# Weight pieces of 1024 columns with two split ahead, in place of pieces of 512 columns with five split ahead

## The chip, the cores and the metric

The kernel runs on one core of one Trainium2 chip. The metric is the device time of one execution in microseconds (us); less is better. TensorE is PE in the profile, VectorE DVE, ScalarE ACT, GpSimd POOL, and SP issues the DMAs.

## The reference

Three residual blocks are applied one after the other to `x` of 256 tokens by 2048 features, all in fp32. What matters here is that each is a long row of products of 256 tokens with big weight matrices, with smaller work between them:

```python
# block 1: gated convolution, gated linear attention (GLA), attention over 256 memory rows
proj = rmsnorm(x) @ w_in                        # 2048 x 19472, cut into 11 parts
y = g0 * (conv @ w_conv_out) + g1 * (gla @ w_gla_out) + g2 * (mem @ w_mem_out)
x = rmsnorm(x + y @ w_out, final_g)
# block 2: sparse attention with a learned top-k, spatial gating, a feed-forward part of 8192
x = x + (...) @ w_out_2
x = rms_norm(x + gelu(rms_norm(x) @ w_ff1) @ w_ff2, final_g_2)
# block 3: latent attention (MLA) and a bidirectional RWKV-7 scan, gated and merged
out = x + rms_norm((...) @ w_out_3, g_post)
```

## The kernel before

**The stream.** All weights of the three blocks lie in DRAM as one stream, in the order in which they are used (`stream_plan`). `cut` cuts each product into pieces: a piece is `n` chunks of 128 rows by `w` columns (512 as a rule), with `n = min(nk, ITEM // w)`; `ITEM` is the number of columns that a piece takes in each partition. Pieces are packed into units of up to `UNIT = 1024` columns (512 KB); one DMA brings one unit into one of `RAW = 4` buffers `raw`.

**The split.** PE multiplies in a fast fp32 form that keeps fewer bits, so each fp32 operand is split into a high and a low part and three products are made: high by high, low by high, high by low. For each piece ACT copies `raw` to `wh` (the high part), and then DVE computes `wl = raw - wh`. The activations were split earlier, into `xh` and `xl` (`yr`, `qa`, `kv` and others in some products). A chunk of 128 x 512 weights then takes 6 matmuls of 512 columns on PE (3 products for 2 halves of the tokens), or 12 of 256 columns in products whose output is wanted transposed (`DIRECT`).

**What runs ahead.** `run_stream` goes through the pieces. At the start of piece `i` it writes the splits up to piece `i + LEAD` into the programs of ACT and DVE, then the evacuation of the product that just ended (`finish`), then the matmuls of piece `i`. `wh` and `wl` come from a pool of `LEAD + 1` buffers each, so the split of piece `i + LEAD` goes into the buffer that piece `i - 1` has just left:

```python
        self.w_p = pool("w", LEAD + 1)
...
            while ns < len(items) and ns <= i + min(LEAD, 1 + i):
...
                wh = self.w_p.tile([128, ITEM], F32R, name="wh", tag="wh")
                wl = self.w_p.tile([128, ITEM], F32R, name="wl", tag="wl")
                nc.scalar.activation(out=wh[:, :size], in_=src, func=AF.Copy)
                nc.vector.tensor_tensor(
                    out=wl[:, :size], in0=src, in1=wh[:, :size].bitcast(F32), op=ALU.subtract
                )
...
            self.finish(over)
```

**The side work.** Everything else (norms, convolution, attention, scans) consists of generators. Between the matmuls `pump` takes a step of each generator that is due. A clock kept by the program at build time (`Issue`), with a cost for each instruction, says what is due; `BACKLOG` bounds how far ACT and DVE may fall behind PE in it. Each engine runs its program strictly in the order in which it was written, so a split stands behind all side work and evacuations that were written before it.

Names used below: `wo` is the last product of block 1, `wo2` the output product of block 2's first part, `f20` to `f23` the feed-forward's second product, `wo3` the last product; `bm`, `br0` and `br1` are the merging products of block 3. Four column blocks (0 to 3) make one product of 2048 columns. The evacuations of `wo` and of `f23` add the residual, and per half of the tokens DVE adds, ACT squares and sums (`junk`), DVE multiplies by a gain row and ACT squares and sums again.

Of the kernel before, what the change touches and what calls it, by code (L numbers as in the profile page):

```python
# [16 lines left out]
AX = mybir.AxisListType  # L17
D = 2048
EPS = 1e-6
ITEM = 512  # L20
UNIT = 1024
NSLOT = 13
RAW = 4
COMMON = ("ev", "sg", "row", "junk", "rsq", "rsz", "ss")
BEGIN = {"qi": 2, "qa": 3}
EXTRA = {1: 0, 2: 0, 3: 1}
LEAD = 5
BACKLOG = 7.7
TABLES = {AF.Exp: ("exp", "ln"), AF.Ln: ("ln",), AF.Sigmoid: ("sigmoid",), AF.Silu: ("silu",), AF.Sqrt: ("sqrt",),
          AF.Gelu_apprx_tanh: ("gelu",), AF.Tanh: ("exp", "sigmoid", "silu", "gelu")}  # L30
# [87 lines left out]
def cut(plan):  # L118

    items, units, off = [], [], 0  # L120
    for key, j, src, row0, nk, col0, w in plan:
        n = min(nk, ITEM // w)
        for k in range(0, nk, n):
# [174 lines left out]
class Builder:  # L298
    def __init__(self, ctx, tc, dram, blocks):
# [7 lines left out]
        self.raw_p = pool("raw", RAW)  # L307
        self.w_p = pool("w", LEAD + 1)
        self.wk = pool("work")
# [183 lines left out]
    def run_stream(self):  # L493
# [5 lines left out]
        for i, it in enumerate(items):  # L499
            self.cur = f"{it.key}{it.j}"  # L500
            opens = it.key in BEGIN and it.first and it.j == 0
            if opens:
                self.finish(over)
                over = None
                self.begin(BEGIN[it.key])
            while ns < len(items) and ns <= i + min(LEAD, 1 + i):
                jt = items[ns]
                while nd < len(units) and nd <= jt.unit + RAW - 1:
                    off, size = units[nd]
                    t = self.raw_p.tile([128, UNIT], F32, name="raw", tag="raw")  # L510

                    m = size if nd else min(size, ITEM)
                    src = wfl[off:off + 128 * size].rearrange("(p n) -> p n", p=128)
# [7 lines left out]
                src = raw[jt.unit][:, jt.uoff:jt.uoff + size]  # L521
# [3 lines that stand above are left out]
# [2516 lines left out]
```

## Time and profile before

| | |
|---|---|
| median of 3 runs | 3540.02 us (3539.14 to 3540.11) |
| the profiled execution | 3546.78 us, span 3545.0 us |
| PE busy | 3506.3 us, 99% of the span |
| DVE busy | 2442.9 us, 69% |
| ACT busy | 1893.6 us, 53% |
| POOL busy | 158.8 us, 4% |
| mean granted PE clock | 0.994 of full speed |
| HBM | 661.74 MB read, 36.73 MB written, 197 GB/s |

The span reaches from the first instruction to the last; the profiled execution has 1.8 us beside it. Busy is the time in which an engine executed something. Consecutive matmuls overlap in the records, so their spacing, not their duration, is what one costs.

### The profile page before, as it was taken

What the parts mean: (1) busy time and instruction counts of PE and PEld (TensorE: products, weight loads), DVE (VectorE), ACT (ScalarE), POOL (GpSimd) and SP (SyncE); (2) the same over time, 40 slices, a digit from 0 to 9 for tenths busy, and PEclk for the clock granted to TensorE, in tenths of its full rate; (3) what the DMA queues carried; (4) which work ended last, traced back from release to release, by engine and by line L of the source; (5) the groups of instructions that cost most, each with busy time, mean ns of one, the idle gap of its engine ahead of it and who ended that gap; (6) DMA issues with size and microseconds to landing.
All of it is one profiled execution on the core that took longest, in us unless ns stands there. A gap on an engine that the chain in (4) does not pass through costs nothing.

```text
span 3545.0 us, 55751 instructions
## 1 busy us (share of the span) xinstructions
PE 3506.3 (99%) x20370; PEld 3036.2 (86%) x20370; DVE 2442.9 (69%) x4447; ACT 1893.6 (53%) x3398; POOL 158.8 (4%) x153
## 2 busy tenths in 40 slices
PE   8999999999999999999999999999999999999998
PEld 7889988888988899988878989898988997787777
DVE  7598898887576666555766555555567578678785
ACT  6555556556454555655445545454555664464444
POOL 1000010001000000100110000000000010000010
PEclk9999999999999999999999999999999999999999
DMA  6555656676677765566665555555575456655665
GB/s 230 169 188 161 188 158 208 193 232 194 181 231 221 239 207 189 178 214 224 215 225 184 185 191 185 194 184 192 187 222 175 147 183 191 217 188 189 230 215 183
DMA packets 235995, 698.98 MB, mean 197 GB/s; under 512 B 44932, under 2 KB 55348, under 8 KB 234056
## 3 DMA queue, kind: packets, MB, share of 16 engines
q1 hardware_dynamic: 235720, 695.43, 60.9%
q8 instruction: 159, 2.61, 0.3%
q14 instruction: 116, 0.95, 0.1%
HBM read 661.74 MB, written 36.73 MB: 197 GB/s over the span
## 4 chain that ended last, share of the span: by engine, by line
PE 91%; DVE 5%; DMA 2%; issue 1%; ACT 1%; SPq 0%; POOL 0%; DVEq 0%; ACTq 0%
PE acc L285 84%; PE bank L285 7%; DVE wl L285 2%; DVE tmp L285 1%; DMA raw<-in_wstream_dram 1%; DVE m L285 0%; ACT wh L285 0%; DMA x<-f 0%; DMA tl<-td 0%; DVE tl L285 0%; DVE rb L285 0%; ACT junk L285 0%; DVE o L285 0%; DVE xl L285 0%; DMA row<-in_rows_dram 0%
## 5 line engine op out<-in xcount | busy, mean ns | idle before, releaser
L285 DVE TENSOR_TENSOR wl<-raw,wh 128x512 fp32r<-128x512 f32 x2290 | 1568.8, 702 | 993.9 <-ACT wh L285 977.1
L285 ACT ACTIVATE wh<-raw 128x512 fp32r<-128x512 f32 x2290 | 1424.2, 630 | 1503.7 <-PE acc L285 936.1
L285 PE MATMUL acc<-wh,xh 128*128 128x512 f32 x3328 | 1324.7, 398 | 11.3 <-ACT xh L285 4.5
L285 PE MATMUL acc<-wh,xl 128*128 128x512 f32 x3328 | 1299.7, 391 | 3.9 <-DVE xl L285 3.9
L285 PE MATMUL acc<-wl,xh 128*128 128x512 f32 x3328 | 1298.8, 390 | 1.2 <-DVE wl L285 1.2
L285 PEld LDWEIGHTS acc<-wh,xh 128*128 128x128 f32 x3328 | 627.5, 189 | 145.9 <-issue 11.9
L285 PEld LDWEIGHTS acc<-wh,xl 128*128 128x128 f32 x3328 | 627.0, 188 | 137.3 <-DVE xl L285 4.7
L285 PEld LDWEIGHTS acc<-wl,xh 128*128 128x128 f32 x3328 | 628.3, 189 | 129.9 <-DVE wl L285 7.0
L285 PE MATMUL acc<-xh,wh 128*128 128x256 f32 (+3 forms) x2224 | 637.7, 287 | 0.0
L285 PE MATMUL acc<-xh,wl 128*128 128x256 f32 (+3 forms) x2224 | 629.6, 283 | 0.0
L285 PE MATMUL acc<-xl,wh 128*128 128x256 f32 (+3 forms) x2224 | 629.6, 283 | 0.0
L285 PEld LDWEIGHTS acc<-xh,wh 128*128 128x128 f32 (+3 forms) x2224 | 423.9, 191 | 3.2 <-issue 2.0
L285 PEld LDWEIGHTS acc<-xl,wh 128*128 128x128 f32 (+3 forms) x2224 | 424.1, 191 | 1.3
L285 PEld LDWEIGHTS acc<-xh,wl 128*128 128x128 f32 (+3 forms) x2224 | 423.8, 191 | 0.4
L285 DVE SCALAR_TENSOR_TENSOR cacc<-u,cvec,cacc 128x226 f32<-128x226 f32 (+28 forms) x464 | 188.5, 468 | 0.0
L285 ACT ACT_TABLE_LOAD x46 | 59.0, 1283 | 3.2 <-DVE mmx L285 1.6
L285 PE MATMUL acc<-wh,yr 128*128 128x512 f32 x128 | 43.7, 410 | 2.0 <-DVE yr L285 2.0
L285 ACT ACTIVATE junk<-x 128x512 bf16<-128x512 f32 x40 | 25.3, 632 | 37.1 <-DVE x L285 36.7
L285 PE MATMUL bank<-ar,bk 64*128 64x128 f32 (+1 forms) x384 | 40.4, 329 | 0.1
L285 POOL TENSOR_TENSOR crstd<-crstd,u 128x256 f32<-128x256 f32 x14 | 21.9, 1561 | 356.5 <-DVE u L285 356.0
L285 PEld LDWEIGHTS bank<-ar,bk 64*128 64x128 f32 x384 | 25.6, 186 | 14.2 <-issue 10.0
L285 POOL MEMSET ropes<- 64x256 f32 x2 | 0.6, 306 | 727.3 <-DVE wl L285 727.2
(427 smaller groups left out, 2205.2 us busy)
## 6 DMA issues: line engine op xcount, KB each, us to landing
raw<-in_wstream_dram SPq DMA_DIRECT2D x1133, 512.0 KB, 3.9
gate<-sg SPq DMA_DIRECT2D x40, 256.0 KB, 2.3
row<-in_rows_dram SPq DMA_DIRECT2D x38, 256.0 KB, 4.8
sg<-gate SPq DMA_DIRECT2D x24, 256.0 KB, 2.9
sg<-z SPq DMA_DIRECT2D x24, 256.0 KB, 2.6
z<-sg SPq DMA_DIRECT2D x20, 256.0 KB, 2.5
f<-x SPq DMA_DIRECT2D x16, 256.0 KB, 2.5
gt<-gate SPq DMA_DIRECT2D x16, 256.0 KB, 4.3
```

Source lines behind the costliest of these rows:

```text
L285: r = f(*a, **k)
```

## The change

`ITEM` goes from 512 to 1024 and `LEAD` from 5 to 2. A piece of a 512-column product is now 2 chunks, takes one ACT and one DVE instruction of 1024 columns, and holds 12 matmuls of 512 columns (24 of 256). The `wh` and `wl` buffers are 3 each of 1024 columns in place of 6 each of 512: the same space. Units, `raw` buffers and matmuls stay as they are. One more place reads `ITEM`: the first unit was loaded by two DMAs of 512 columns each and is now loaded by one.

```diff
-ITEM = 512
+ITEM = 1024
 UNIT = 1024
 NSLOT = 13
 RAW = 4
...
-LEAD = 5
+LEAD = 2
 BACKLOG = 7.7
```

DVE, at the evacuation of `wo`'s column block 0 (`acc` is the product in PSUM, `x` the new residual, `row` the gain), before:

```order
L285 TENSOR_TENSOR xl<-bank_11936,xh 128x512
L285 TENSOR_TENSOR wl<-raw,wh 128x512 x11
L285 TENSOR_TENSOR x_11871<-acc_11875,x_11871 128x512
L285 TENSOR_TENSOR x_11871<-x_11871,row 128x512
L285 TENSOR_TENSOR x_11872<-acc_11876,x_11872 128x512
L285 TENSOR_TENSOR x_11872<-x_11872,row 128x512
L285 TENSOR_TENSOR wl<-raw,wh 128x512 x8
```

The same place of DVE's program after the change:

```order
L285 TENSOR_TENSOR xl<-bank_10350,xh 128x512
L285 TENSOR_TENSOR wl<-raw,wh 128x1024 x5
L285 TENSOR_TENSOR x_10290<-acc_10294,x_10290 128x512
L285 TENSOR_TENSOR x_10290<-x_10290,row 128x512
L285 TENSOR_TENSOR x_10291<-acc_10295,x_10291 128x512
L285 TENSOR_TENSOR x_10291<-x_10291,row 128x512
L285 TENSOR_TENSOR wl<-raw,wh 128x1024 x4
```

The evacuation is the same. The last split ahead of it covers 1024 columns and belongs to the piece two further on; before it covered 512 and belonged to the piece five further on.

PE, where the RWKV scan of block 3 ends (`vy` is its last output, transposed by PE for the product `br1`; `yr` the input of `br0` and `br1`), before:

```order
L285 MATMUL acc_34821<-wl,yr_33946 128x512
L285 MATMUL acc_34821<-wh,yr_33946 128x512
L285 MATMUL bank_34844<-cst_80,vy 128x128 x4
L285 MATMUL acc_34820<-wh,yr_33946 128x512
L285 MATMUL acc_34820<-wl,yr_33946 128x512
```

The same transposes on PE after the change:

```order
L285 MATMUL acc_30144<-wl,xh 128x512
L285 MATMUL acc_30144<-wh,xh 128x512
L285 MATMUL bank_30217<-cst_80,vy 128x128 x4
L285 MATMUL acc_30145<-wh,xh 128x512
L285 MATMUL acc_30145<-wl,xh 128x512
```

They stood within `br0`'s last column block and stand now within `bm`'s column block 2: counted over the whole of PE's program, 111 stream matmuls earlier. Most of the scan moves forward like this, by 15 to 111 matmuls, and the end of the convolution by 270 to 285, since the build-time clock books less time on ACT and DVE for the splits.

SP, at the start of the program, before:

```order
L285 DMA cvec_92<-in_cvec_dram 128x32
L285 DMA raw<-in_wstream_dram 128x512 x2
L285 DMA xin<-in_memT_dram 128x1024
L285 DMA raw<-in_wstream_dram 128x1024 x2
L285 DMA xin<-in_memT_dram 128x1024
```

SP at the start after the change:

```order
L285 DMA cvec_92<-in_cvec_dram 128x32
L285 DMA raw<-in_wstream_dram 128x1024
L285 DMA xin<-in_memT_dram 128x1024
L285 DMA raw<-in_wstream_dram 128x1024 x2
L285 DMA xin<-in_memT_dram 128x1024
```

The first two half units have become one DMA; nothing else moved there.

## Rows read from the trace of the kernel before

**Rows 1.** The page's first part: busy time (share of the span) and instructions.

```profile
PE 3506.3 (99%) x20370; PEld 3036.2 (86%) x20370; DVE 2442.9 (69%) x4447; ACT 1893.6 (53%) x3398; POOL 158.8 (4%) x153
```

**Rows 2.** The page's chain that ended last, by engine.

```profile
PE 91%; DVE 5%; DMA 2%; issue 1%; ACT 1%; SPq 0%; POOL 0%; DVEq 0%; ACTq 0%
```

**Rows 3.** Waits of PE: total us, times, longest.

```profile
PE acc L285 <- ACT xh L285: 4.5, 1, 4.5
PE acc L285 <- DVE xl L285: 3.9, 1, 3.9
PE acc L285 <- issue: 3.6, 1, 3.6
PE acc L285 <- ACT wh L285: 3.2, 1, 3.2
PE acc L285 <- DVE yr L285: 2.0, 2, 1.8
```

**Rows 4.** Groups by form: busy us, mean ns, then idle before them.

```profile
L285 DVE TENSOR_TENSOR wl<-raw,wh 128x512 fp32r<-128x512 f32 x2270 | 1557.6, 703 | 979.2 <-ACT wh L285 962.4 <-PE acc L285 5.8
L285 ACT ACTIVATE wh<-raw 128x512 fp32r<-128x512 f32 x2270 | 1413.7, 630 | 1491.9 <-PE acc L285 926.4 <-DVE wl L285 470.9 <-DMA raw<-in_wstream_dram 41.3
...
L285 ACT ACTIVATE x<-x 128x1024 f32<-128x1024 f32 x8 | 8.2, 1048 | 0.0
...
L285 DVE TENSOR_TENSOR sq<-sq 128x1024 f32<-128x1024 f32 x3 | 3.7, 1219 | 0.0
```

**Rows 5.** Timeline, an undisturbed piece: start us, duration us, engine.

```profile
1842.20 0.39 PE L285 MATMUL acc<-wh,xh 128*128 128x512 f32 x1
1842.40 0.63 ACT L285 ACTIVATE wh<-raw 128x512 fp32r<-128x512 f32 x1 [0.73 <-DVE wl L285]
...
1843.06 0.69 DVE L285 TENSOR_TENSOR wl<-raw,wh 128x512 fp32r<-128x512 f32 x1 [0.67 <-ACT wh L285]
...
1849.22 0.39 PE L285 MATMUL acc<-wl,xh 128*128 128x512 f32 x1
```

**Rows 6.** Timeline, the evacuation of `wo`'s column block 0.

```profile
1197.89 0.63 ACT L285 ACTIVATE wh<-raw 128x512 fp32r<-128x512 f32 x1 [0.73 <-DVE wl L285]
...
1199.16 0.68 DVE L285 TENSOR_TENSOR x<-acc,x 128x512 f32<-128x512 f32 x1
...
1204.23 1.14 ACT L285 ACTIVATE wh<-raw 128x512 fp32r<-128x512 f32 x2
...
1204.88 1.29 DVE L285 TENSOR_TENSOR wl<-raw,wh 128x512 fp32r<-128x512 f32 x2 [1.31 <-ACT wh L285]
...
1206.08 0.39 PE L285 MATMUL acc<-wl,xh 128*128 128x512 f32 x1
```

**Rows 7.** Timeline, DVE: the first and the last of its 2290 `wl` instructions.

```profile
7.13 0.69 DVE L285 TENSOR_TENSOR wl<-raw,wh 128x512 fp32r<-128x512 f32 x1 [5.61 <-ACT wh L285]
...
3526.12 0.69 DVE L285 TENSOR_TENSOR wl<-raw,wh 128x512 fp32r<-128x512 f32 x1 [0.67 <-ACT wh L285]
```

**Rows 8.** Timeline, the start of the program.

```profile
9.40 0.63 ACT L285 ACTIVATE wh<-raw 128x512 fp32r<-128x512 f32 x1 [2.31 <-DMA raw<-in_wstream_dram]
...
11.43 0.80 PE L285 MATMUL acc<-wh,xh 128*128 128x512 f32 x1 [4.47 <-ACT xh L285]
...
29.79 0.50 PE L285 MATMUL acc<-wh,xl 128*128 128x512 f32 x1 [3.91 <-DVE xl L285]
```

**Rows 9.** Timeline around 3051 us (PE) and in the scan's end (PE).

```profile
3055.44 0.59 PE L285 MATMUL acc<-wh,xh 128*128 128x512 f32 x1 [3.60 <-issue]
...
3419.23 0.72 PE L285 MATMUL acc<-wh,yr 128*128 128x512 f32 x2 [1.77 <-DVE yr L285]
```

**Rows 10.** Windows: busy us of each engine, then PEclk, the granted clock, DMA.

```profile
1225.00:1232.00 7.00, 7.00 (x33) 5.75 (x32) 5.00 (x8) 4.97 (x11) 0.00 (x0) 1.00 0.71 209
...
3310.00:3325.00 15.00, 13.06 (x304) 10.06 (x304) 9.17 (x14) 6.59 (x12) 0.00 (x0) 1.00 0.77 214
3410.00:3425.00 15.00, 12.99 (x53) 9.75 (x52) 14.07 (x20) 5.32 (x9) 5.97 (x4) 0.89 0.71 228
```

## The prediction, made before the result was known

> **What bounds the kernel now.** I read the page from the top. The first part has PE busy for 3506.3 us, 99% of the span, while DVE (69%) and ACT (53%) have room [rows 1]. The chain of work that ended last says the same: 91% of it is PE [rows 2]. So the time is PE's own work plus the 38.7 us of the span in which PE was not busy (3545.0 - 3506.3), and the waits name that rest: two at the start of the program, one for instructions, one for `wh`, two for `yr`, all others shorter [rows 3]. PE's matmuls are the same before and after. The change can therefore act in two ways only: by taking away some of these waits, or by making new ones. The saving on DVE and ACT themselves is off the path.
>
> That saving is real. A 512-column split costs 703 ns on DVE and 630 ns on ACT; 128x1024 instructions of the same kind take 1219 and 1048 ns [rows 4]. Two old splits for one new one save 0.19 us of DVE and 0.21 us of ACT, over some 1145 pairs about 215 and 243 us. It shortens nothing by itself, since PE does not wait for the mean load of either engine.
>
> **What is late next.** What the change costs is distance. In an undisturbed stretch a piece of 6 matmuls begins at 1842.20; ACT then splits the piece five further on from 1842.40, DVE is done with it at 1843.75, and PE reads that `wl` at 1849.22, so it is ready 5.47 us early [rows 5]. From 1842.20 to 1849.22 PE issues 31 matmuls (five pieces of 6 and one more), 0.2265 us each, so a piece takes 1.36 us. After the change the split is for the piece two further on, and two pieces of 12 matmuls are 5.44 us, not 6.80. The split takes ACT 1.05 and DVE 1.22 in series, not 0.63 and 0.69. The same sum: 0.20 + 1.05 + 0.02 + 1.22 = 2.49 us after the piece's start, needed at 5.44 + 0.23 = 5.67. It is still 3.2 us early. In a quiet stretch the change costs nothing and PE's own work covers it. Nor do the boundaries between pieces cost PE anything now: the 31 matmuls span five of them at an even pace, so halving their number gains nothing.
>
> The reserve shrinks where side work is queued ahead of a split. The clearest place is the evacuation of `wo` [rows 6]. The piece starts at 1197.7; the split written before the evacuation is done at 1199.25, then DVE and ACT alternate until 1204.3, the next `wh` starts at 1204.23, its `wl` ends at 1204.88 + 0.69 = 1205.57, and PE needs it at 1206.08: 0.51 us to spare. After the change the piece after that evacuation is needed at the same moment (three pieces of 2.72 us where there were six of 1.36). But the split ahead of the evacuation takes 0.42 us more on ACT and 0.52 more on DVE, so everything behind starts 0.94 later, and the split behind it takes 0.94 more again. 0.51 - 1.88 = -1.4: PE waits 1.4 us. Where the queue is on DVE alone the loss is the same by another way: 1.36 of window and 0.52 of duration, 1.88.
>
> So the question is how often less than 1.9 us is to spare now. I paired each of the 2290 `wl` instructions with the matmul that first reads it (first and last in [rows 7]). Half have 5.47 us or more. 56 have under 1.9, at 26 places; the shortfalls from 1.9, the largest at each place, sum to 29.4 us. By kind:
>
> - Evacuations of `wo` and `f23`, 8 places: 11.5 us (1.1 to 1.85 each). The order shows them unchanged. I take all of it.
> - Nine single places (two in the GLA products, three in the gates, one each in the top-k, `us`, `wo2` and `wo3`): 6.0 us. The order keeps them near where they are. I take all.
> - RWKV scan, 8 places: 10.6 us. Here the order moves side work by 15 to 111 matmuls, so these coincidences are dealt anew, with lighter engines. Bounds 0 and 10.6; I take half, 5.3.
> - The first 30 us, one place, 1.3 us, replaced by the next term.
>
> A rule speaks against this change here, and it fits these places: the Trainium skill (Perfetto Trace Analysis, Optimizing Scalar/DVE Operations) says that grouping work into larger operations helps throughput where the engine is saturated, and that where Scalar and Vector are not saturated but cause bubbles on others, breaking instructions up may let work finish sooner. By its first half the 215 us of DVE would count, by its second the 1.4 us at each evacuation; the 69% and 53% of rows 1 put this kernel under the second.
>
> **The start.** PE's first product waits for `xh`, behind the second half-unit split that starts at 9.40 and begins at 11.43; then PE waits 3.9 us more for an `xl` until 29.79 [rows 8]. Now the first `wh` needs the whole first unit (9.4) and runs to 10.4, the second needs a second unit that before was first touched later. PE starts 1 to 4 us later; but the `xl` that ends the second wait stands, by the order, behind 5 new splits instead of 12 old, so much of that wait goes. Bounds -4 and +3; I take +1.
>
> **Waits that go.** The scan's last transposes stand 111 matmuls, some 25 us, earlier, so the waits for `yr` (2.0 us in all [rows 3], the longer in [rows 9]) should go: -2.0. The 3.6 us for instructions [rows 9] have nothing to do with splits; I leave them.
>
> DMAs: the same units through the same four buffers. A unit's buffer is free one split earlier or later by half a microsecond, and units are issued about 8 us ahead both times; nothing is taken for it.
>
> **Sum.** 11.5 + 6.0 + 5.3 + 1.0 - 2.0 = +21.8 us. Against the profiled execution, 3546.8 us (span 3545.0, 1.8 beside it), that is 3568.6. This execution lay 6.8 us above the median of the runs; against the median of 3540.0 the forecast is **3562 us**.
>
> **The rivals.**
>
> *No change.* The lateness stays inside PE's slack: the moved side work and the lighter engines take away the small queues, and only the evacuations remain. 11.5 x 1/2 - 2.0 = +4, 3544 us. For it: 215 us less on DVE. Against: the eight evacuations are chains between ACT and DVE in which lightness doesn't count.
>
> *Faster.* The place is the dense scan of block 3 and the program's start. If side results come early enough to remove all waits that side work causes there (`xl` 3.9, `yr` 2.0, and, an estimate, some 5 us in shorter ones of the 38.7), and reserves hold elsewhere, the time falls by 11 to 3529 us. It decides at 1.9 us: if the new reserve is only 1 us smaller than the old at these places, the shortfall falls to about 10.6 and is balanced. Against it: rows 6 leave no other arithmetic for the eight evacuations.
>
> *Slower by twice as much: the clock.* The 15 us from 3410, in which PE was idle for 2.01 us, have a mean granted clock of 0.89: for part of them PE ran at the lower of its two levels (1.2 in place of 2.4 GHz), and 1.65 us of full-speed work were lost. The 15 us from 3310, with 1.94 us idle, kept 1.00, and so does an evacuation of `wo` now, without idle time [rows 10]. If each of the 13 places with 1.39 us or more did so, 21 us would be added: 3583 us. The Trainium skill (TensorE: Matmul & The Clock Gate, What's actually happening) says that recent activity sets the granted clock, which is the way this rival goes; rows 10 have a case for and a case against.
>
> **How the numbers follow.** Chances: the forecast (faintly to clearly slower, 3548 to 3575) 0.55; the clock or a denser queue 0.15; no change 0.20; faster 0.10. A measurement of this kernel tells about 0.2%, 7 us, from no change. So slower 0.70, same 0.20, faster 0.10. The range runs from 3537, inside the no-change case, to 3587, past the clock case; the forecast's own range is 3548 to 3575.
>
> **What would show it.** DVE and ACT busy lower by about 215 and 243 us; in the waits of PE, `wh` and `wl` with some 20 us together, where `wh` has 3.2 now [rows 3]; a wait of 1.4 us at PE's fourth piece after each evacuation of `wo` and `f23`; no more wait for `yr`. Quiet stretches would keep `wl` some 3.2 us early. I am wrong if these evacuations show PE unbroken, if 1024-column splits take longer than 1.05 and 1.22 us, or if PE's waits fall on side results in place of splits.

## The result and the profile after

The changed kernel takes **3576.1 us** (median of 4 runs, 3568.1 to 3580.1) against 3540.1 us (3539.1 to 3540.1): a ratio of 1.0098, 95% interval 1.0086 to 1.0110, 36 us slower. The forecast was 3562 us, range 3537 to 3587. The sign and the main mechanism were right, the size was 14 us short. The profiled execution took 3574.1 us, its span 3572.4.

The page's first part and its chain that ended last, by engine, against [rows 1, 2]:

```profile
PE 3515.4 (98%) x20370; PEld 3035.0 (85%) x20370; DVE 2300.9 (64%) x3303; ACT 1690.6 (47%) x2255; POOL 166.3 (5%) x153
PE 87%; DVE 6%; ACT 2%; DMA 2%; issue 2%; POOL 0%; SPq 0%; POOLq 0%; DVEq 0%; ACTq 0%
```

DVE is busy 142 us less and ACT 203 us less, and the kernel is slower: two lighter engines, neither of them the bound. On the chain PE lost 4 points, and ACT and DVE gained one each. PE's waits (total us, times, longest) say to whom, against [rows 3]; the last two rows are those of the weight loads that run ahead of the matmuls:

```profile
PE acc L285 <- DVE wl L285: 18.2, 29, 0.9
PE acc L285 <- ACT wh L285: 7.8, 13, 2.7
PE acc L285 <- ACT xh L285: 7.4, 1, 7.4
PE bank L285 <- ACT w L285: 2.4, 1, 2.4
...
PEld acc L285 <- DVE wl L285: 28.9, 33, 1.2
...
PEld acc L285 <- ACT wh L285: 13.4, 14, 3.1
```

The waits for `wl` and `wh` rose from 1.2 and 3.2 us to 18.2 and 7.8. There are 29 for `wl`, none longer than 0.9 us: many small latenesses, one at a place. `yr` and the 3.6 us for instructions are gone from the list, and the `xl` of the start is down to 0.2; the one wait for `xh` grew.

The split instructions by form (busy us, mean ns of one, idle before), against [rows 4]:

```profile
L285 DVE TENSOR_TENSOR wl<-raw,wh 128x1024 fp32r<-128x1024 f32 x1135 | 1397.2, 1236 | 1149.5 <-ACT wh L285 1146.6
L285 ACT ACTIVATE wh<-raw 128x1024 fp32r<-128x1024 f32 x1135 | 1198.4, 1059 | 1664.2 <-PE acc L285 1428.0 <-issue 102.5 <-DMA raw<-in_wstream_dram 62.4
```

1.24 and 1.06 us each, where 1.22 and 1.05 were taken. An undisturbed piece, against [rows 5] (timeline: start us, duration, engine):

```profile
2097.24 0.39 PE L285 MATMUL acc<-wh,xh 128*128 128x512 f32 x1
...
2097.44 1.06 ACT L285 ACTIVATE wh<-raw 128x1024 fp32r<-128x1024 f32 x1 [1.66 <-PE acc L285]
...
2098.53 1.23 DVE L285 TENSOR_TENSOR wl<-raw,wh 128x1024 fp32r<-128x1024 f32 x1 [1.50 <-ACT wh L285]
...
2102.91 0.39 PE L285 MATMUL acc<-wl,xh 128*128 128x512 f32 x1
```

`wl` is ready at 2099.76 and first read at 2102.91: 3.15 us early, where 5.47 was measured before and 3.2 forecast. PE runs through it without a break. Now the evacuation of `wo`'s column block 0, against [rows 6]:

```profile
1205.15 1.06 ACT L285 ACTIVATE wh<-raw 128x1024 fp32r<-128x1024 f32 x1 [1.66 <-PE acc L285]
...
1206.24 1.23 DVE L285 TENSOR_TENSOR wl<-raw,wh 128x1024 fp32r<-128x1024 f32 x1 [1.49 <-ACT wh L285]
...
1207.38 0.68 DVE L285 TENSOR_TENSOR x<-acc,x 128x512 f32<-128x512 f32 x1
...
1212.36 0.19 ACT L285 ACTIVATION_READ_ACCUMULATOR junk<-x 128x1 f32 x1
...
1212.45 2.94 ACT L285 ACTIVATE wh<-raw 128x1024 fp32r<-128x1024 f32 x3
1212.88 0.39 PE L285 MATMUL acc<-wh,xl 128*128 128x512 f32 x1
1213.53 2.36 DVE L285 TENSOR_TENSOR wl<-raw,wh 128x1024 fp32r<-128x1024 f32 x2 [1.74 <-ACT wh L285]
1213.55 0.50 PE L285 MATMUL acc<-wh,xh 128*128 128x512 f32 x1 [0.28 <-ACT wh L285]
1214.81 0.50 PE L285 MATMUL acc<-wl,xh 128*128 128x512 f32 x1 [0.76 <-DVE wl L285]
```

The reader should follow the queue: the first `x<-acc` stands behind the split that ends at 1207.47, ACT and DVE alternate until 1212.36, and only then does the next `wh` begin. PE gets it at 1213.55, 0.67 us after it began its last product at 1212.88, where 0.23 is its pace, and then `wl` 1.26 us later. 0.44 + 1.03 = 1.5 us are lost (1.4 forecast). The 1.03 is one DVE split less one matmul. The same 1.26 us between the two starts stand at 13 places of the program, seven of the eight evacuations among them; at the other late places less is lost. The page counts only 0.28 and 0.76 as idle, since the modelled end of a matmul lies behind the next one's start; so the sum of named waits is less than the loss.

### Where along the program the time goes

The weight stream is 17208 matmuls into `acc`, in the same order in every kernel here. So the start times of the n-th of them can be compared. The table gives them for the kernel before (profiled a second time, see below) and how much later they come in the others. Up to each mark all kernels have issued the same number of side matmuls (but for four transposes at 6212, which the changed kernel and those made from it issue later). In the dense part of block 3, behind 14616, only the end is comparable.

| n-th | before, 2nd profile | before, 1st | changed | halves_b1024 | halves_evac | i512_l4 | after_bl65 | before_bl65 |
|---|---|---|---|---|---|---|---|---|
| 1246 (start over) | 308.9 | +0.7 | -2.1 | -1.4 | -2.2 | -1.8 | -2.9 | +1.1 |
| 4302 (`k`, `q`, gates) | 932.7 | -0.8 | +6.4 | +0.5 | +6.4 | +4.8 | +4.4 | -0.1 |
| 5448 (up to `wo`) | 1158.5 | -0.8 | +6.4 | +0.5 | +6.4 | +4.8 | +4.4 | -0.1 |
| 6212 (`wo` over) | 1306.6 | -0.8 | +11.1 | -0.1 | +6.8 | +8.6 | +9.0 | -0.1 |
| 8886 (`wo2` over) | 1864.1 | +4.7 | +22.6 | +7.9 | +20.7 | +17.3 | +19.5 | +3.0 |
| 13470 (up to `f23`) | 2578.3 | +4.7 | +22.6 | +7.9 | +20.7 | +18.2 | +19.5 | +3.0 |
| 14300 (`f23` over) | 2749.6 | +4.9 | +30.9 | +9.2 | +23.4 | +22.1 | +26.2 | +3.1 |
| 14616 (up to the scan) | 2810.5 | +4.9 | +30.8 | +9.2 | +23.4 | +22.1 | +26.2 | +3.1 |
| 17207 (end) | 3523.5 | +9.7 | +37.0 | +18.6 | +30.9 | +33.1 | +31.3 | +21.5 |

The changed kernel loses nothing over the 700 us of quiet stream (8886 to 13470), 4.7 us in `wo`, 8.3 in `f23`, 8.5 from the start to the end of the gates, 11.5 in the first part of block 2, 6.2 in block 3, and it gains 2.1 at the start.

These figures are no better than the two profiles of before agree, and one program's two executions differ by 5.5 us in the first part of block 2 and by 4.8 in block 3. Against the first profile, from which the prediction was read, the changed kernel loses 10.0 us up to the gates, 4.7 in `wo`, 6.0 in the first part of block 2, 8.1 in `f23` and 1.4 in block 3, and gains 2.8 at the start: 27.3 in all.

### The profile page after: what moved, and what is told of

The parts are those of the page before. It is cut to its first block, busy times and chain, and to the rows that moved or that the text cites. A ratio compares the mean times of both kernels' runs of the same rounds, so it can differ in the third digit from the quotient of the medians.

```text
span 3572.4 us, 52077 instructions
## 1 busy us (share of the span) xinstructions
PE 3515.4 (98%) x20370; PEld 3035.0 (85%) x20370; DVE 2300.9 (64%) x3303; ACT 1690.6 (47%) x2255; POOL 166.3 (5%) x153
## 4 chain that ended last, share of the span: by engine, by line
PE 87%; DVE 6%; ACT 2%; DMA 2%; issue 2%; POOL 0%; SPq 0%; POOLq 0%; DVEq 0%; ACTq 0%
PE acc L285 80%; PE bank L285 7%; DVE wl L285 2%; DMA raw<-in_wstream_dram 1%; ACT wh L285 1%; ACT junk L285 1%; DVE tmp L285 1%; DVE x L285 0%; DMA tl<-td 0%; DVE sg L285 0%; DVE m L285 0%; DMA x<-f 0%; DMA sg<-z 0%; DVE tl L285 0%; ACT L285 0%
## 5 line engine op out<-in xcount | busy, mean ns | idle before, releaser
L285 DVE TENSOR_TENSOR wl<-raw,wh 128x1024 fp32r<-128x1024 f32 x1146 | 1407.5, 1233 | 1161.8 <-ACT wh L285 1159.0
L285 ACT ACTIVATE wh<-raw 128x1024 fp32r<-128x1024 f32 x1146 | 1207.0, 1057 | 1675.3 <-PE acc L285 1433.4
L285 PE MATMUL acc<-wh,xh 128*128 128x512 f32 x3328 | 1326.0, 398 | 15.2 <-ACT wh L285 7.8
L285 PE MATMUL acc<-wh,yr 128*128 128x512 f32 x128 | 41.3, 394 | 0.0
L285 PEld LDWEIGHTS bank<-ar,bk 64*128 64x128 f32 x384 | 25.6, 187 | 15.2 <-issue 9.2
```

Source lines behind the costliest of these rows:

```text
L285: r = f(*a, **k)
```

## The experiments

**Theory 1**, that of the prediction: the look-ahead is shorter in time (5.44 us in place of 6.80) and a split is longer in series (2.29 us in place of 1.33); wherever other work is queued ahead of a split, PE waits. **Theory 2**: the clock that orders the side work books less for the larger splits, so side work stands elsewhere, by bad luck worse. **Theory 3**: the longer instruction as such costs. A trace shows where PE waits, but not which of the three made it; the runs take them apart.

**halves_b1024: the same order and distance, shorter instructions.**

```
for a in range(0, size, 512):
    e = min(a + 512, size)
    real.scalar.activation(out=wh[:, a:e], in_=src[:, a:e], func=AF.Copy)
    real.vector.tensor_tensor(out=wl[:, a:e], in0=src[:, a:e], ...)
clock.take("ACT", "activation", (src,), {})       # booked as one of 1024
clock.take("DVE", "tensor_tensor", (src,), {})
```

> The changed kernel with each split issued as two 512-column pairs (ACT, DVE, ACT, DVE), still pieces of 1024 columns, two ahead, and the clock told one 1024-column split, so that the order of the side work is that of the changed kernel. Theory 1: in a quiet stretch the first half of wl is ready 0.20 + 0.63 + 0.02 + 0.69 = 1.54 us after the piece before begins its own, needed at 5.67, so 4.1 us early in place of 3.2; at the first evacuation of wo what stands behind starts 0.7 us later than in the kernel before and not 0.94, and its own first half takes no longer than before: 0.51 - 0.7 = -0.2, a wait of 0.2 us where the changed kernel has 1.5. Over the eight evacuations 2 us in place of 11.5; in all 3540 to 3556 us. Theory 2 (order of the side work): the order is kept, so the time stays at 3566 to 3584 us.

3554.3 us (3551.3 to 3557.9), 1.0038 (1.0025 to 1.0050) of before. The time lies in theory 1's range. The instructions of PE, ACT and DVE stand in the changed kernel's order, but that each split is two pairs. Its waits, and the same evacuation of `wo`:

```profile
PE acc L285 <- DVE wl L528: 6.5, 16, 1.0
...
PE acc L285 <- ACT wh L527: 2.8, 3, 1.9
```

```profile
1206.15 3.22 ACT L527 ACTIVATE wh<-raw 128x512 fp32r<-128x512 f32 x6
1206.80 3.70 DVE L528 TENSOR_TENSOR wl<-raw,wh 128x512 fp32r<-128x512 f32 x6 [1.31 <-ACT wh L527]
...
1207.17 0.39 PE L285 MATMUL acc<-wh,xh 128*128 128x512 f32 x1
1207.55 0.50 PE L285 MATMUL acc<-wl,xh 128*128 128x512 f32 x1
```

The work between the splits takes as long as in the changed kernel, but behind it the first half of `wl` ends 1.3 us after its `wh` begins (0.65 to the start of `wl`, and 0.69) instead of 2.3, and PE loses 0.15 us (0.38 less 0.23), not 1.5. Of the 36.0 us 13.4 are left, so 22.6 hang on the length of one split instruction, with the order untouched; theory 2 alone falls. The table says where: up to the gates this kernel loses 1.9 us where the changed one loses 8.5, but in the first part of block 2 still 8.0 of 11.5, which the length does not explain. The rule that the prediction took from the Trainium skill (Perfetto Trace Analysis, Optimizing Scalar/DVE Operations), that breaking instructions up may let work be completed sooner where Scalar and Vector are not saturated but cause bubbles on other engines, agrees with this run's 22.6 us.

**halves_evac: halves only around `wo` and `f23`.**

```
cuts = 512 if jt.key in ("wo", "f23") or it.key in ("wo", "f23") else size
```

> The changed kernel, with 512-column halves only for the splits that are issued while pieces of wo and f23 are multiplied, or are of them; all others stay 1024 columns in one instruction, and the order of the side work is kept. Theory 1: the eight evacuations, where the changed kernel lost 4.6 us around wo and 8.1 around f23 against the kernel before, wait 0.2 us each in place of 1.5; 8 x 1.3 = 10 us less than the changed kernel, 3561 to 3571 us, with the other late places (gates, k and q, the scan) as they were. Theory 2 (order of the side work): no change, 3570 to 3582 us. Theory 3 (the longer instruction costs evenly everywhere): these places hold about a tenth of all splits, so 2 us, 3570 to 3580 us.

3568.0 us (3562.8 to 3570.0), 8.1 less than the changed kernel. In the table it follows the changed kernel within 0.1 us as far as `wo`; there it loses 0.4 in place of 4.7, and in `f23` 2.7 in place of 8.3. That is 9.9 us less at the eight evacuations, of the 10 expected.

**i512_l4 and i512_l3: shorter distance, old instructions** (`LEAD = 5` to 4, and to 3).

> The kernel before with pieces of 512 columns, four ahead in place of five: the distance alone falls by 1.36 us, to the 5.44 us of the changed kernel, while the split instructions stay at 630 and 703 ns. Theory 1: reserve in a quiet stretch 4.1 us; the places with less than 1.36 us to spare in the kernel before (20 places) lack 17.7 us in all, so 3547 to 3562 us, between the two kernels. Theory 2 (booking and order of the side work): the clock books the same as in the kernel before, so 3540 to 3547 us. Theory 3 (it is the serial length of the 1024-column split alone): 3540 to 3545 us.

> The kernel before with pieces of 512 columns, three ahead in place of five: reserve in a quiet stretch 5.47 - 2.72 = 2.75 us, less than the 3.2 of the changed kernel. Theory 1: 31 places have less than 2.72 us to spare in the kernel before and lack 49 us in all, so 3570 to 3600 us, as slow as the changed kernel or slower. Theory 2 (booking and order): 3540 to 3550 us. Theory 3 (length of the split alone): 3540 to 3550 us.

3565.1 us (3562.4 to 3569.8) and 3616.4 us (3612.7 to 3624.2); both above their ranges. Four ahead, then three ahead:

```profile
PE acc L285 <- DVE wl L285: 13.8, 22, 2.5
PE acc L285 <- ACT wh L285: 6.4, 8, 3.9
```

```profile
PE acc L285 <- DVE wl L285: 38.6, 56, 4.7
PE acc L285 <- ACT wh L285: 21.7, 15, 4.7
```

With the old split instructions a shorter distance makes the same kind of waits; theory 3 alone falls too. But the order is not that of the kernel before: counted in the traces, 207 and 228 of some 430 groups of side matmuls (a group is alike ones in a row) stand elsewhere in the stream, so the whole time of these two runs holds distance and order together. Distance by itself shows at the evacuations, where DVE has the same instructions between two splits: with four ahead they lose 3.8 us in `wo` and 3.9 in `f23`. The arithmetic of the prediction, what the places lack once each has lost so much, orders all four kernels, but is low each time:

| kernel | each place loses | places lack in all | measured |
|---|---|---|---|
| halves_b1024 | 0.7 us | 5.4 us | +13.4 us |
| i512_l4 | 1.36 | 17.7 | +24.2 |
| changed | 1.9 | 29.4 | +36.0 |
| i512_l3 | 2.72 | 49 | +75.5 |

(5.4 is worked out in the same way as the others. The 0.7 us hold for the evacuations only. By the prediction's other way, where the queue is on DVE alone, a place loses the 1.36 us of window in halves_b1024 too, which makes about 12 of the 5.4.) i512_l4 and the changed kernel lie 6.5 us above, i512_l3 26; why it is so much there is open, but in its profile 30 us are lost behind 14616, in block 3.

**booked512: the changed kernel with a dearer booking.**

```
real.scalar.activation(out=wh[:, :size], in_=src, func=AF.Copy)     # one of 1024, as changed
real.vector.tensor_tensor(out=wl[:, :size], in0=src, ...)
for a in range(0, size, 512):
    part = src[:, a:min(a + 512, size)]
    clock.take("ACT", "activation", (part,), {})
    clock.take("DVE", "tensor_tensor", (part,), {})
```

> The changed kernel with its 1024-column split instructions and two pieces ahead as they are, but the clock that orders the side work is told the cost of two 512-column splits, as in the kernel before. Theory 1 (the loss is the shorter distance plus the longer serial split, paid wherever other work is queued ahead of a split): the instructions that cost the time are untouched, so the time stays at 3566 to 3584 us, PE waits for wl some 15 to 22 us, and the 0.76 us wait for wl behind the first evacuation of wo stays. Theory 2 (the loss comes from the side work that the cheaper booking moved): most of the 36 us goes, 3540 to 3552 us, and the waits for wl fall below 8 us.

3656.7 us (3650.5 to 3659.7): both expectations missed. The waits for `wl` and `wh` are 14.5 and 7.8 us, about what theory 1 had (15 to 22 for `wl`); the rest is new:

```profile
PE bank L285 <- DVE tl L285: 29.4, 2, 28.1
PE acc L285 <- DVE wl L526: 14.5, 21, 2.6
PE bank L285 <- DVE vy L285: 12.1, 1, 12.1
```

The scan at the program's end comes too late for the stream: PE stands 28.1 and 12.1 us for its results. The edit does not give the old booking. In the kernel before each split of 512 columns is booked on its own. Here the two of a piece stand in one chain, and the clock starts the second ACT copy only behind the first DVE subtraction: by the costs in `Issue`, 0.62 + 0.1 + 0.61 + 0.1 + 0.62 = 2.0 us of ACT's time in place of 2 x 0.62 = 1.2. ACT and DVE are booked full sooner than in either kernel, and side work is held back more. So the run does not isolate the booking's part as it was meant to. It shows two things: the order has a price of its own, at another place than the splits; and with nearly all of the side work moved (401 of some 430 groups) the wait behind the first evacuation of `wo` is still 0.76 us, as theory 1 had it.

**after_bl9, after_bl65, before_bl65: other orders** (`BACKLOG = 7.7` to 9.0 or 6.5: how far ahead of PE the engines may be booked before side work is held back). Counted in the traces and without buffer numbers, 26, 161 and 171 of some 430 groups of side matmuls stand elsewhere in the stream than in their parent; the larger counts in two of the expectations are of rows with buffer numbers. The change itself moves 335.

> The changed kernel with another order of the side work and the same split instructions and distance: the side work is admitted until ACT or DVE is booked 9.0 us ahead of PE in place of 7.7. Theory 1: the splits have the same reserve; queues of side work ahead of them are a little longer, so 3570 to 3590 us, waits for wl and wh 24 to 34 us. Theory 2 (the changed kernel lost by an unlucky order of the side work): the order is dealt anew and the time falls clearly, 3545 to 3565 us.

> The changed kernel with the side work admitted until ACT or DVE is booked 6.5 us ahead of PE in place of 7.7. This moves far more of the side work than 9.0 did (some 3100 of 18023 PE rows against some 900). Theory 1 (reserve and length of the split): the time stays near the changed kernel, 3566 to 3590 us, with waits for wl and wh of 22 to 32 us. Theory 2 (an unlucky order): the order is dealt anew and most of the loss goes, 3540 to 3560 us.

> The kernel before with the same change of the admission of side work, 6.5 us in place of 7.7 (it moves some 3800 of 18023 PE rows). Theory 1 (the long reserve of the kernel before swallows most queues, whatever the order): 3535 to 3546 us, waits for wl and wh under 7 us. Theory 2 (the order is what counts, and that of the kernel before was a lucky one): 3550 to 3570 us. If the smaller backlog is simply better for both kernels, it takes the 13 us off that it took off the changed one, 3527 us, and beats both.

after_bl9: 3576.1 us, waits for `wl` and `wh` 18.1 and 8.2, as theory 1; it is a weak test with so few groups moved. after_bl65: 3562.8 us (3562.0 to 3567.8), between both theories, while its waits for `wl` and `wh`, 19.6 and 6.7, are as theory 1 had them. before_bl65: 3558.9 us (3555.8 to 3560.2), outside theory 1's range and within theory 2's. Its waits:

```profile
PE bank L285 <- DVE vy L285: 10.7, 2, 10.1
PE bank L285 <- DMA ev<-yd: 6.4, 1, 6.4
...
PE acc L285 <- ACT wh L285: 2.9, 1, 2.9
PE acc L285 <- DVE wl L285: 2.5, 5, 1.1
```

`wl` and `wh` stay at 5.4 us (under 7, as theory 1 said); the 18 us are again mostly scan results that come late. The table separates the two: up to the scan before_bl65 is 3.1 us behind, and after_bl65 26.2. Up to there the changed pieces lose in both orders; behind it before_bl65 loses 18.4 us and after_bl65 5.1. With 6.5 on both sides the change costs only 3.9 us (3562.8 against 3558.9), because there the old pieces pay for the late scan. So theory 1 held for the waits for splits, and theory 2 for the whole time.

**before_again and before_ramp: a second profile, and the start alone.**

```
-            while ns < len(items) and ns <= i + min(LEAD, 1 + i):
+            while ns < len(items) and ns <= i + min(LEAD, 1 + i, 3 + i // 16):
```

> The kernel before, profiled once more, to see whether its first profiled execution (3546.8 us, 6.8 above the median) was typical. If it was the one odd run, this one takes 3539 to 3543 us and has some 6 us less between PE's matmuls, most of it in the last 700 us; then a like-for-like comparison with the changed kernel gives 34 us in place of 27. If a profile as such costs 6 us, it takes 3545 to 3548 us again.

> The kernel before, but while the first 48 pieces are multiplied the look-ahead grows from three pieces to five (one more for every 16 pieces), so that fewer splits stand ahead of the first xl. The start term by itself: the changed kernel and the one with three pieces ahead have PE at the same product 2.8 and 4.2 us earlier 43 us after the start. Theory 1: PE's 3.9 us wait for xl at 25.9 us goes and the time falls by 2.5 to 4 us, 3536 to 3539 us; behind it nothing changes. If the first splits were late instead, the gain would be lost: 3540 to 3545 us.

before_again took 3537.1 us. The first profile lost 5.5 us more around 1860 and 4.8 more in block 3. Neither is typical: 15 other executions of the kernel before in that comparison took 3537.5 to 3547.0 us, 3541.8 in the middle, so the two stand at both ends. The changed kernel's profile lies 27.3 us behind the one and 37.0 behind the other; the medians say 36.0. before_ramp: 3539.3 us against 3541.8, ratio 0.9991 (0.9982 to 1.0000), not told apart from no change, though its trace is 2.8 us ahead of before_again at 1246; the wait for `xl` in [rows 8] shrinks and comes earlier:

```profile
27.90 0.50 PE L285 MATMUL acc<-wh,xl 128*128 128x512 f32 x1 [2.25 <-DVE xl L285]
```

**i1024_l3_r2 and i512_l6_r3: more distance, paid with raw buffers** (1024 columns, `LEAD` 3, `RAW` 2; 512 columns, `LEAD` 6, `RAW` 3).

> The changed kernel with its 1024-column splits in one instruction, three pieces ahead in place of two; the space comes from the raw buffers, two in place of four. Theory 1: the reserve in a quiet stretch grows from 3.15 to 5.9 us, more than the 5.47 of the kernel before, and the evacuation of wo has 2.72 us more and 1.0 of it used by one more split ahead: waits for wl and wh fall from 26 us to under 6, and the time to 3536 to 3552 us, if two raw buffers are enough: a raw buffer is free when its split is done, its load takes 3.6 us, and the next split into it stands 5.4 us later, so 1.8 us are left in a quiet stretch; behind evacuations splits would wait for the load and some of the gain would be lost, up to 3560 us. Theory 2 (order): the order is dealt anew with the same booking, 3560 to 3590 us. Theory 3 (length of the split alone): 3570 to 3582 us.

> The kernel before with 512-column pieces six ahead in place of five, the space from one raw buffer less (three in place of four). Theory 1: reserve 6.8 us in a quiet stretch; only the 4.4 us of waits for wl and wh that the kernel before has can go, so 3535 to 3541 us, the same within what can be told. If three raw buffers are too few, splits wait for loads: 3545 us or more. Theory 2 (order): dealt anew, 3530 to 3550 us.

4021.4 us and 3580.8 us, the first far above every range, the second where it was expected if three buffers are too few (3545 or more). ACT's waits for loads, first in the one, then in the other:

```profile
ACT wh L285 <- DMA raw<-in_wstream_dram: 1772.3, 821, 15.5
```

```profile
ACT wh L285 <- DMA raw<-in_wstream_dram: 333.4, 174, 8.8
```

The changed kernel has 62.4 us there and the kernel before 41.3. In the first run PE then waits 78.0 us for `wl` and 55.1 for `wh`: a split that waits for its load is late however early it was issued. In the second it is not the splits: PE waits 1.1 us for `wl`, and up to the scan the run is 15.2 us behind before_again, at the end 39.0, with 12.5 us of waiting for `vy` and 7.0 for `tl`, again results of the scan. Neither run says what distance alone would give back. No kernel here beats the one before by more than can be told.

## Why the prediction was right, and where it was too small

**What bounds the kernel** held: PE 98%, quiet stretches untouched, the lighter engines worth nothing. DVE fell by 142 us and ACT by 203, not 215 and 243. The step that failed there took 1219 ns from another instruction (1236 measured, some 19 us over 1135 splits) and multiplied mean durations; instructions back to back overlap (six of 703 ns in 3.70 us, above), and the pages' busy time of the `wl` group fell by 161 us (1568.8 to 1407.5). The other 19 us on DVE were not followed up.

**The evacuations**: 11.5 us forecast, 4.7 + 8.3 = 13.0 measured, and the one worked through 1.5 us in place of 1.4. Shown by halves_b1024 and halves_evac; booked512 has the same wait in another order.

**The nine single places**: 6.0 us forecast; the two stretches in which they lie (`wo3`, in block 3, left out) lost 20.0 us against the second profile (8.5 up to the gates, 11.5 in block 2), 16.0 against the first. This term was mis-sized, and the step at fault is "the order keeps them near where they are". In the gates the short places of before lacked 0.07, 0.34 and 0.34 us; the changed kernel is late at others too, as here in the first gate:

```profile
539.13 2.94 ACT L285 ACTIVATE wh<-raw 128x1024 fp32r<-128x1024 f32 x3
540.22 2.36 DVE L285 TENSOR_TENSOR wl<-raw,wh 128x1024 fp32r<-128x1024 f32 x2 [3.45 <-ACT wh L285]
540.24 0.50 PE L285 MATMUL acc<-wh,xh 128*128 128x512 f32 x1 [0.50 <-ACT wh L285]
541.50 0.50 PE L285 MATMUL acc<-wl,xh 128*128 128x512 f32 x1 [0.76 <-DVE wl L285]
```

ACT had been occupied with side work to 539.13, from 535.92 on with a table load, two steps of the GLA and two sums. In the kernel before three splits stand ahead of that table load. So a place that has more than 1.9 us to spare in one order is late in another, and counting only the places now short gives too little.

In block 2 only a part of the 11.5 us is the splits': 2.8 us come at `v2`, with a late split. 3.6 come at `us`, where PE waits for a side result, `at`, and runs at a lower clock behind it. 4.6 come at `wo2`, where the kernel before itself loses 5.5 us more in its first profile than in its second, with a lower clock again. The changed kernel's waits for `at` and its 15 us there (busy us of each engine, then PEclk, the granted clock):

```profile
PE bank L285 <- DVE at L285: 1.9, 3, 1.0
```

```profile
1770.00:1785.00 15.00, 13.31 (x60) 10.74 (x59) 12.08 (x17) 4.72 (x6) 5.81 (x4) 0.89 0.68 232
```

The kernel before at `wo2`, its first profile, then its second:

```profile
1860.00:1875.00 15.00, 14.44 (x54) 11.51 (x54) 9.52 (x16) 8.95 (x17) 0.00 (x0) 0.77 0.54 176
```

```profile
1860.00:1875.00 15.00, 15.00 (x71) 12.44 (x70) 10.36 (x18) 8.70 (x16) 0.00 (x0) 1.00 0.72 239
```

The first profile of before waits 0.8 us for `at` and halves_b1024 2.9. So the longer waits go with the changed order and not with the length of a split; the prediction had left side results out of this stretch.

**The scan and `yr`**: 5.3 - 2.0 = 3.3 forecast, 6.2 measured against the second profile and 1.4 against the first; `yr` did go. How much of it is order and how much splits is not settled.

**The start**: +1 forecast, -2.1 measured, within its bounds. PE's first product came 3.0 us later (11.43 to 14.45, behind a whole unit's load), but the 3.9 us for `xl` went. So did a lower clock behind that wait: in the 15 us from 30 the granted clock is 0.89 and 0.92 in the two profiles of before, 1.00 in the changed kernel and in before_ramp. That the start gained where the sum has +1 hid 3 us of what the other terms lack, by luck.

**Clock.** It was a rival, and part of it is there: 15-us windows of the changed kernel, against [rows 10]:

```profile
1205.00:1220.00 15.00, 13.96 (x65) 11.02 (x64) 7.80 (x9) 8.39 (x15) 0.00 (x0) 1.00 0.61 191
...
1870.00:1885.00 15.00, 11.60 (x42) 8.94 (x41) 5.87 (x7) 5.13 (x9) 0.00 (x0) 0.77 0.65 247
2595.00:2610.00 15.00, 13.40 (x54) 10.36 (x53) 7.93 (x15) 6.88 (x13) 0.00 (x0) 0.89 0.58 177
```

At `wo2` (1870) PE was idle for 3.4 us and 15 x 0.23 = 3.5 us of full-speed work were lost; at `f23` 1.7; at `wo` none. Summed in this way between the first and the last matmul of the stream, the clock costs 13.7 us in the changed kernel, 16.4 in the first profile of before and 10.9 in the second. So 2.8 of the 37.0 us are the clock's, not the 21 of the rival, and 5.5 of the 9.7 us between the two profiles of before.

Of the 36 us, then, 22.6 are shown to hang on the instruction length at the same order and distance. The other 13.4 come with distance and the new order together. At the evacuations i512_l4 shows the distance's part, and at `us` halves_b1024 shows one of the order's; elsewhere the two are not told apart, since i512_l4 has a third order. A version with the changed pieces in exactly the old order was not tried.

## What to carry to other kernels

Larger pieces in the same space cost a look-ahead twice: fewer microseconds between issue and need, and a longer series ahead of the need. Work out the reserve that is left (here 5.47 to 3.15 us), look for the chains between engines that stand ahead of a refill, and price the places that are nearly short too, not only those that are. Where an order of side work is set by booked costs, try the change at more than one setting of the order before judging it: here it cost 36 us at one and 4 at another. And take the unchanged kernel's profile twice before a stretch of the program is blamed: here two of them differed by 9.7 us.

## What was not expected of the hardware

The changed kernel's runs spread over 12 us where those of the kernel before lay within 1 in the same comparison; in a later comparison 15 runs of the kernel before spread over 9.5, so this is not the change's doing alone. The clock answers to PE's pauses unevenly: 1.00 around the evacuation above with 1.04 us of idle time, 0.89 around one of `f23` with 1.60, and in booked512, where PE waits for the scan, the lower of its two levels (0.50) over a whole window:

```profile
3420.00:3435.00 15.00, 7.50 (x34) 5.48 (x32) 9.92 (x36) 0.56 (x3) 0.00 (x0) 0.50 0.22 70
```
